# Three of the first tile's four repeat copies on VectorE and one on ScalarE, in a kernel that normalizes rows and writes each twice

## The chip, the cores and the metric

The kernel runs on one core of a Trainium2 chip. Its time is the device time of one execution in microseconds, and the median of several executions is given. A profiled execution also has a span, from the first to the last instruction that the profiler records; the time is a little longer than the span.

## The reference

```python
def setup_inputs():
    B, S, D = 8, 512, 2048
    R = 2
    return {
        "x": np.random.randn(B, S, D).astype(np.float32),
        "gamma": np.random.randn(D).astype(np.float32),
    }

def reference(x, gamma):
    B, S, D = x.shape
    x_rep = np.repeat(x, 2, axis=1)
    rms = np.sqrt((x_rep ** 2).mean(axis=-1, keepdims=True) + 1e-6)
    x_norm = x_rep / rms
    return (x_norm * gamma[None, None, :]).astype(np.float32)
```

Each of the 8 x 512 = 4096 rows of 2048 numbers is divided by its root mean square and multiplied by `gamma`, and the result is written twice, to two neighbouring rows of the output. The input is 33.55 MB, the output 67.11 MB, both in 32-bit floats.

## The kernel before

**Tiles.** The input is read in four loads. A load gives each of the 128 partitions 8 neighbouring rows (8.39 MB). It feeds two tiles of K = 4 rows a partition. The output of a tile is 8 rows a partition, since each row stands there twice, and leaves in one store of 8.39 MB. That makes 4 loads and 8 stores.

**Space.** One buffer `y` holds 24 rows a partition, in three parts of 8: `first` at 0, `second` at 8, `third` at 16. A load into row 4 fills the upper half of `first` and the lower half of `second`; a load into `third` fills that. Each tile is scaled from where it was loaded into rows 0, 2, 4 and 6 of the part that its store will read, and the copies then fill rows 1, 3, 5 and 7.

**Order.** The work is written out by hand, and each engine takes its instructions in the order of the program. `four(n, m, ...)` handles one group: two loads and four tiles with their stores. It is called twice, for loads 0 and 1 and for loads 3 and 2. All loads and stores are issued by SyncE on one queue, one after another, and SyncE waits in turn for what each of them needs: a store for the copies that fill its part, a load or a later tile's scaling for the store that still reads the part. In the first group both loads are issued at once; in the second they are issued as earlier stores land. In each group the queue then holds, in order, load, load, store, store, store, store.

**One tile.** ScalarE squares each row and sums it (`squares`, line 69), then takes the root for the tile or half of it (line 73). VectorE takes the reciprocal (line 82) and multiplies each row by it and by `gamma` in one instruction (`scale`, line 83). `repeat(to, k0, k1, copy)` (lines 88 to 90) copies rows k0 to k1 of the tile into the rows beside them with a single instruction of whichever engine it is given; its shape is (k1 - k0) rows of 2048. `store` (line 56) sends the 8 rows.

**Who copies.** In the first tile of a group (lines 103 to 107) the rows are squared and scaled in two halves; ScalarE copies rows 0 and 1, VectorE rows 2 and 3, and the first store follows. The second tile (lines 108 to 111) is scaled from its last row to its first; ScalarE copies rows 2 and 3, VectorE rows 0 and 1. Then ScalarE squares both tiles of the other load and makes their copies alone (lines 112 to 119). In the first group the second half's reciprocals are taken row by row (`at_once` = 1), in the second both at once.

**The end.** After the last group ScalarE waits until the last but one store has landed and then makes three copies on one partition (line 156); SyncE waits for the last store.

Of the kernel before, what the change touches and what calls it, by code (L numbers as in the profile page):

```python
# [1 line left out]

# [4 lines left out]


@with_exitstack
def kernel(  # L10
    ctx: ExitStack,
    tc: tile.TileContext,
    x: bass.AP,
    gamma: bass.AP,
    out: bass.AP,
):
    nc = tc.nc
    P = nc.NUM_PARTITIONS
    f32 = mybir.dt.float32
    Act = mybir.ActivationFunctionType  # L20
    Alu = mybir.AluOpType

    B, S, D = x.shape
    Bo, So, Do = out.shape
    R = So // S
    assert R == 2 and D == Do and B == Bo and So == S * R
    eps = 1e-6
    inv_d = 1.0 / float(D)


    K = 4
    N = B * S
    ntiles = N // (P * K)
    assert N % (P * K) == 0 and ntiles == 8
    H = 2
    x_t = x.rearrange("b s d -> (b s) d").rearrange("(n p k) d -> n p k d", p=P, k=H * K)
    out_t = out.rearrange("b s d -> (b s) d").rearrange("(n p h j) d -> n h p (j d)", p=P, h=H, j=K * R)

    singles = ctx.enter_context(tc.tile_pool(name="singles", bufs=1))
    rows = ctx.enter_context(tc.tile_pool(name="rows", bufs=1))  # L40
    junk = ctx.enter_context(tc.tile_pool(name="junk", bufs=1, space=bass.MemoryType.PSUM))
    small = ctx.enter_context(tc.tile_pool(name="small", bufs=4))

    y = nc.alloc_sbuf_tensor("y", [P, 3 * K * R, D], f32)
    first, second, third = 0, K * R, 2 * K * R

    def load(n, at):
        nc.sync.dma_start(out=y[:, at : at + H * K, :], in_=x_t[n])  # L50

    landed = [nc.alloc_semaphore(f"landed{h}") for h in range(H)]
    passed = nc.alloc_semaphore("passed")

    def store(n, h, to, own=False):
        dma = nc.sync.dma_start(
            out=out_t[n, h], in_=y[:, to : to + K * R, :].rearrange("p j d -> p (j d)")
        )
        if own:
            tc.no_tile_sem_insts.add(dma.ins.name)  # L60
            dma.then_inc(landed[h], 16)

    def squares(at, rows):

        n = len(rows)
        ss = small.tile([P, n], f32, name=f"ss{n}")
        for c, k in enumerate(rows):
            sq = junk.tile([P, D], f32, name="sq")
            nc.scalar.activation(  # L69
                out=sq[:], in_=y[:, at + k, :], func=Act.Square, accum_out=ss[:, c : c + 1]  # L70
            )
        rms = small.tile([P, n], f32, name=f"rms{n}")
        nc.scalar.activation(out=rms[:], in_=ss[:], func=Act.Sqrt, scale=inv_d, bias=eps_t[:])  # L73
        return rms

    def scale(at, to, rows, rms, at_once=K):
        n = len(rows)
        rstd = small.tile([P, n], f32, name=f"rstd{n}")
        for c, k in enumerate(rows):
            if c % at_once == 0:  # L80
                part = slice(c, min(c + at_once, n))
                nc.vector.reciprocal(out=rstd[:, part], in_=rms[:, part])  # L82
            nc.vector.scalar_tensor_tensor(  # L83
                out=y[:, to + R * k, :], in0=y[:, at + k, :], scalar=rstd[:, c : c + 1],
                in1=gamma_b[:], op0=Alu.mult, op1=Alu.mult,
            )

    def repeat(to, k0, k1, copy):
        y_r = y[:, to + R * k0 : to + R * k1, :].rearrange("p (k r) d -> p k r d", r=R)
        copy(out=y_r[:, :, 1, :], in_=y_r[:, :, 0, :])  # L90

    ctx.enter_context(tc.manual_schedule())

    half = K // 2
    up, down = list(range(K)), list(range(K - 1, -1, -1))

    def four(n, m, constants, at_once, last=False):


        load(n, first + K)  # L100
        constants()
        load(m, third)
        for rows, n_at_once in ((up[:half], half), (up[half:], at_once)):
            scale(first + K, first, rows, squares(first + K, rows), n_at_once)
        repeat(first, 0, half, nc.scalar.copy)
        repeat(first, half, K, nc.vector.tensor_copy)
        store(n, 0, first)
        scale(second, second, down, squares(second, down))
        repeat(second, half, K, nc.scalar.copy)
        repeat(second, 0, half, nc.vector.tensor_copy)  # L110
        store(n, 1, second)
        roots = [squares(third + h * K, up) for h in range(H)]
        scale(third, first, up, roots[0])
        repeat(first, 0, half, nc.scalar.copy)
        repeat(first, half, K, nc.scalar.copy)
        store(m, 0, first, last)
        scale(third + K, third, up, roots[1])
        repeat(third, 0, K, nc.scalar.copy)
        store(m, 1, third, last)

    gamma_b = singles.tile([P, D], f32, name="gamma_b")
    G, E = 16, 3
    C = D // G - E
    gamma_s = y[0:1, 0:2, :].rearrange("p k (c d) -> p (k c) d", c=G // 2)
    gamma_t = y[0:1, 2, :]
    eps_t = singles.tile([P, 1], f32, name="eps_t")

    def constants():
        nc.gpsimd.memset(eps_t, eps)  # L129

        nc.scalar.activation(out=gamma_s[0:1, 0, :1], in_=eps_t[0:1, :], func=Act.Sqrt)  # L131
        nc.scalar.dma_start(
            out=gamma_s[0:1, :, :C],
            in_=gamma[: G * C].rearrange("(p c d) -> p c d", p=1, c=G),
        )
        for c in range(E):
            at = G * C + c * G
            nc.scalar.dma_start(
                out=gamma_t[0:1, c * G : (c + 1) * G],
                in_=gamma[at : at + G].partition_broadcast(1),  # L140
            )
        nc.gpsimd.partition_broadcast(  # L142
            out_ap=gamma_b[:, : G * C].rearrange("p (c d) -> p c d", c=G),
            in_ap=gamma_s[0:1, :, :C],
        )
        nc.gpsimd.partition_broadcast(out_ap=gamma_b[:, G * C :], in_ap=gamma_t[0:1, : E * G])  # L146

    four(0, 1, constants, 1)
    four(3, 2, lambda: None, half, last=True)

    ctx.close()
    tc.close()
    tc.compile()
    nc.scalar.wait_ge(landed[0], 16).then_inc(landed[0], -16)  # L154
    for a, b in ((0, K), (K, 2 * K), (2 * K, 2 * K + 2)):
        done = nc.scalar.copy(out=y[0:1, a:b, :], in_=y[0:1, a:b, :])  # L156
    done.then_inc(passed, 1)
    nc.vector.wait_ge(passed, 1).then_inc(passed, -1)
    nc.sync.wait_ge(landed[1], 16).then_inc(landed[1], -16)


# [1 line left out]
_INS = ['x', 'gamma']  # L163
_OUTS = [((8, 1024, 2048), 'float32')]


# [23 lines left out]
```

## Time and profile before

| What | Value |
|---|---|
| median of 3 runs | 236.88 us (236.84 to 237.99) |
| profiled execution, time | 237.09 us |
| profiled execution, span | 235.8 us |
| VectorE busy | 84.4 us (36%) |
| ScalarE busy | 127.6 us (54%) |
| moved by DMA | 100.69 MB, mean 427 GB/s |
| read from HBM, written to it | 33.56 MB, 67.11 MB |
| DMA time from issue to landing, median | stores 24.9 us, loads of x 31.5 us |

How to read it. DVE is VectorE, ACT is ScalarE, SP is SyncE; SPq is SyncE issuing a transfer, and L90 is line 90 of the kernel. A group of instructions is given as line, engine, operation, output <- input with the shape as partitions x elements, and the count; then the busy time in us and the mean of one in ns; then the idle time of the engine just before them and what ended it. A line of the timeline begins with the start and the length in us; a line with x4 merges four instructions, and its length reaches to the end of the last. A line of the windows gives a stretch and its length, the busy time of DVE, ACT and POOL with their counts, the granted clock of TensorE, the share of the 16 DMA engines and the rate. That view books a DMA packet whole in the window in which it starts, so in a very short window the share can be over 1.

### The profile page before, as it was taken

How to read it: one execution, taken by the hardware profiler on the slowest of the kernel's cores; microseconds unless marked ns; L12 is line 12 of the kernel's file. 1: busy time of each engine (PE TensorE's matmuls, PEld its weight loads, DVE VectorE, ACT ScalarE, POOL GpSimd, SP SyncE). 2: the span in 40 equal slices, each digit the busy share in tenths (PEclk: the TensorE clock that was granted, in tenths of full speed). 3: DMA queues.
4: the chain of work that ended last, by engine and by line, in shares of the span. 5: the costliest groups of instructions: out<-in, count | busy, mean ns of one | idle time of the engine just before them, and what ended most of it. 6: DMA issues, size and time to landing. Idle time of an engine off the chain costs nothing. (4 is left out here: it accounts for less than half of the span.)

```text
span 235.8 us, 233 instructions
## 1 busy us (share of the span) xinstructions
DVE 84.4 (36%) x47; ACT 127.6 (54%) x89; POOL 2.9 (1%) x7
## 2 busy tenths in 40 slices
DVE  0000396594599500000000006937928993000000
ACT  2001989479999370000000039891999966502996
POOL 0120000000000000000000000000000000000000
DMA  9898988989898998989899898989889898989988
GB/s 356 357 534 356 534 356 356 534 356 534 356 523 368 411 478 356 534 356 534 356 445 445 356 534 356 534 356 511 378 378 511 356 534 356 523 367 467 423 356 357
DMA packets 1769, 100.69 MB, mean 427 GB/s; under 512 B 231, under 2 KB 231, under 8 KB 231
## 3 DMA queue, kind: packets, MB, share of 16 engines
q1 hardware_dynamic: 1728, 100.66, 99.0%
q14 instruction: 3, 0.02, 0.0%
q10 hardware_dynamic: 38, 0.01, 0.0%
HBM read 33.56 MB, written 67.11 MB: 427 GB/s over the span
## 5 line engine op out<-in xcount | busy, mean ns | idle before, releaser
L69 ACT ACTIVATE sq<-y 128x2048 f32<-128x2048 f32 x32 | 60.1, 1878 | 73.0 <-DMA y<-in_x_dram 72.4
L83 DVE SCALAR_TENSOR_TENSOR y<-y,rstd,gamma_b 128x2048 f32<-128x2048 f32 x32 | 73.8, 2348 | 1.7 <-DMA out_dram<-y 1.2
L90 ACT COPY y<-y 128x4096 f32<-128x4096 f32 (+1 forms) x10 | 42.6, 4283 | 19.2 <-DVE y L83 18.5
L82 DVE RECIPROCAL rstd<-rms 128x4 f32<-128x4 f32 (+2 forms) x11 | 1.8, 168 | 110.1 <-ACT rms L73 110.1
L156 ACT COPY y<-y 1x8192 f32<-1x8192 f32 (+1 forms) x3 | 17.4, 5876 | 13.0 <-ACTq L154 13.0
L90 DVE COPY y<-y 128x4096 f32<-128x4096 f32 x4 | 9.2, 2294 | 0.1
L69 ACT ACTIVATION_READ_ACCUMULATOR sq<-y 128x1 f32 x32 | 6.0, 186 | 0.0
L73 ACT ACTIVATE rms<-ss,eps_t 128x4 f32<-128x4 f32 (+1 forms) x10 | 3.0, 297 | 0.3
L142 POOL PARTITION_BROADCAST gamma_b<-y x1 | 2.2, 2244 | 9.9 <-DMA y<-in_gamma_dram 9.9
L131 ACT ACT_TABLE_LOAD x1 | 1.3, 1283 | 0.7 <-PEq L174 0.7
L146 POOL PARTITION_BROADCAST gamma_b<-y x1 | 0.3, 323 | 10.1 <-DMA y<-in_gamma_dram 10.1
L131 ACT ACTIVATE y<-eps_t 1x1 f32<-1x1 f32 x1 | 0.2, 202 | 0.0
L174 POOL MEMSET const-uint8-127<- 128x1 uint8 x1 | 0.1, 102 | 0.0
L129 POOL MEMSET eps_t<- 128x1 f32 x1 | 0.1, 98 | 0.3 <-POOLq L174 0.3
L174 POOL MEMSET const-bfloat16-1.0<- 128x1 bf16 x1 | 0.1, 101 | 0.0
L174 POOL MEMSET const-float32-0.0<- 128x1 f32 x1 | 0.1, 98 | 0.2 <-issue 0.2
L174 POOL MEMSET const-float32-1.0<- 128x1 f32 x1 | 0.1, 98 | 0.0
## 6 DMA issues: line engine op xcount, KB each, us to landing
out_dram<-y SPq DMA_DIRECT2D x8, 24.9
y<-in_x_dram SPq DMA_DIRECT2D x4, 31.5
y<-in_gamma_dram ACTq DMA_DIRECT2D x3, 0.1 KB
y<-in_gamma_dram ACTq DMA_DIRECT2D x1, 7.8 KB, 8.3
```

Of the source, the lines that this page charges most:

```text
L69: nc.scalar.activation(out=sq[:], in_=y[:, at + k, :], func=Act.Square, accum_out=ss[:, c : c + 1])
L73: nc.scalar.activation(out=rms[:], in_=ss[:], func=Act.Sqrt, scale=inv_d, bias=eps_t[:])
L82: nc.vector.reciprocal(out=rstd[:, part], in_=rms[:, part])
L83: nc.vector.scalar_tensor_tensor(out=y[:, to + R * k, :], in0=y[:, at + k, :], scalar=rstd[:, c : c + 1], in1=gamma_b[:], op0=Alu.mult, op ...
L90: copy(out=y_r[:, :, 1, :], in_=y_r[:, :, 0, :])
L129: nc.gpsimd.memset(eps_t, eps)
L131: nc.scalar.activation(out=gamma_s[0:1, 0, :1], in_=eps_t[0:1, :], func=Act.Sqrt)
L142: nc.gpsimd.partition_broadcast(out_ap=gamma_b[:, : G * C].rearrange("p (c d) -> p c d", c=G), in_ap=gamma_s[0:1, :, :C],)
L146: nc.gpsimd.partition_broadcast(out_ap=gamma_b[:, G * C :], in_ap=gamma_t[0:1, : E * G])
L156: done = nc.scalar.copy(out=y[0:1, a:b, :], in_=y[0:1, a:b, :])
L174: nc = _bacc.Bacc("TRN2", target_bir_lowering=False, num_devices=1)
```

## The change

In `four`, which both groups run, ScalarE copies one row of the first tile (row 0) where it copied two, and VectorE copies three (rows 1 to 3) where it copied two. The number of instructions stays: one copy on each engine. The copies of all other tiles, the order of the program, and the loads and stores stay as they are.

```diff
         for rows, n_at_once in ((up[:half], half), (up[half:], at_once)):
             scale(first + K, first, rows, squares(first + K, rows), n_at_once)
-        repeat(first, 0, half, nc.scalar.copy)
-        repeat(first, half, K, nc.vector.tensor_copy)
+        repeat(first, 0, 1, nc.scalar.copy)
+        repeat(first, 1, K, nc.vector.tensor_copy)
         store(n, 0, first)
```

## The prediction

> **What bounds the kernel now.** I read the page first, then the DMA queues, the windows around two moments, the timeline of VectorE and SyncE there, and the groups by form.
>
> ```profile
> DMA  9898988989898998989899898989889898989988
> q1 hardware_dynamic: 1728, 100.66, 99.0%
> L82 DVE RECIPROCAL rstd<-rms 128x4 f32<-128x4 f32 (+2 forms) x11 | 1.8, 168 | 110.1 <-ACT rms L73 110.1
> ```
>
> The transfers set the time. All loads and stores stand on one queue, q1, and its packets fill 99.0% of 16 engines' span; VectorE alone waits 110 us. No compute can shorten that; compute can only lengthen it, by letting the queue run dry. A store can be late in four places per group, so the question is which one is nearly late now. The windows show it; the columns that matter are the DMA share and the GB/s, and this view books a packet whole at the moment it starts.
>
> ```profile
> 1.70:2.30 0.60, 0.00 (x0) 0.51 (x2) 0.00 (x0) 1.00 5.26 1748
> 39.40:41.30 1.90, 0.00 (x0) 1.87 (x3) 0.00 (x0) 1.00 0.00 0
> 41.30:41.90 0.60, 0.00 (x0) 0.57 (x3) 0.00 (x0) 1.00 4.04 1748
> 155.50:157.40 1.90, 0.00 (x0) 1.87 (x3) 0.00 (x0) 1.00 0.08 34
> 157.40:158.10 0.70, 0.00 (x0) 0.67 (x3) 0.00 (x0) 1.00 3.47 1498
> ```
>
> In 0.6 us 1748 GB/s are 1.05 MB, which is 16 packets of 64 KB, one on each engine. The first line is the start of the first load. Until 41.3 us 16.8 MB have started, which are the two loads of the first group, so the burst at 41.30 to 41.90 is the first packet of the group's first store: the engines come free from the loads there, the first at 41.35. By the same count (8.39 MB a transfer) the burst from 157.44 us is the first packet of the second group's first store. Now when those stores are issued, and what comes just ahead:
>
> ```profile
> 34.54 2.35 DVE L83 SCALAR_TENSOR_TENSOR y<-y,rstd,gamma_b 128x2048 f32<-128x2048 f32 x1
> 36.93 2.29 DVE L90 COPY y<-y 128x4096 f32<-128x4096 f32 x1
> ...
> 153.21 2.29 DVE L90 COPY y<-y 128x4096 f32<-128x4096 f32 x1
> ```
>
> ```profile
> 0.73 0.85 SPq L50 DMA_DIRECT2D y<-in_x_dram  x2
> 39.29 48.30 SPq L56 DMA_DIRECT2D out_dram<-y  x4
> 100.25 20.05 SPq L50 DMA_DIRECT2D y<-in_x_dram  x2
> 155.56 48.25 SPq L56 DMA_DIRECT2D out_dram<-y  x4
> ```
>
> VectorE's copy ends at 39.22 and 155.50, and the store is issued 0.06 to 0.07 us later (39.29, 155.56): VectorE's copy is the last thing the store waits for. The issue leads the engines' coming free by 41.35 - 39.29 = 2.06 us, and by 157.44 - 155.56 = 1.88 us. How much lead an issue needs is seen once, at the start: issue at 0.73, first packets from 1.73, so 1.00 us; that issue took 0.42 us where a store's takes 0.35, so 0.93 for a store. The slack in the two places is therefore about 2.06 - 0.93 = 1.13 and 1.88 - 0.93 = 0.95 us, and a longer VectorE copy goes straight against it.
>
> **The change, part by part.** Its cost hangs on these rows:
>
> ```profile
> L83 DVE SCALAR_TENSOR_TENSOR y<-y,rstd,gamma_b 128x2048 f32<-128x2048 f32 x32 | 73.8, 2348 | 1.7 <-DMA out_dram<-y 1.2
> L90 ACT COPY y<-y 128x4096 f32<-128x4096 f32 x8 | 28.6, 3600 | 11.1 <-DVE y L83 10.4 <-DVE rstd L82 0.7
> L90 ACT COPY y<-y 128x8192 f32<-128x8192 f32 x2 | 14.0, 7017 | 8.0 <-DVE y L83 8.0
> L90 DVE COPY y<-y 128x4096 f32<-128x4096 f32 x4 | 9.2, 2294 | 0.1
> ```
>
> *ScalarE's copy, two rows to one, twice.* Two rows take 3.60 and four 7.02, so a row is 1.71 and one alone 1.89 us. It needs only row 0, which VectorE has finished by 29.7, so the 0.73 us idle before it goes too: it runs from about 31.3 to 33.2 in place of 32.05 to 35.65. ScalarE's next squares start 2.3 us sooner (about 2.4 from 148.35 in the second group), and so does the second store's chain. Worth nothing: that store is ready at 55.8 now and the engines want it only at 60.7, and the first store waits for VectorE, not for ScalarE.
>
> *VectorE's copy, two rows to three, twice.* No copy of three rows, nor of any odd number, is in the trace. A small VectorE instruction costs 0.154 us (the reciprocal of 128x1), so a two-row copy is 0.15 fixed and 2.14 of streaming. Lower end: time goes by elements at the rate of the two-row copy, 0.15 + 1.5 x 2.14 = 3.36 (3.44 with nothing fixed). Upper end: an odd count loses the fast rate, 0.15 + 3 x 2.14 = 6.57. Between them: a two-row copy (2294 ns) takes no longer than the multiply of one row (2348 ns), so the engine seems to move two rows side by side, at one element each a cycle; a third row then has no partner and needs a pass of its own, 0.15 + 2 x 2.14 = **4.43 us**. I take this: it explains why two rows cost what one does without supposing that one row could be cut in two.
>
> [...]
>
> *The first store, first group.* Copy from 36.93 to 41.36, issue at 41.43, first packet 0.93 later at 42.36; the engines come free at 41.35: **1.0 us** idle on each. *Second group.* Copy 153.21 to 157.64, issue 157.70, packet 158.63 against 157.44: **1.2 us**. The first stall delays the second group's loads, the compute that waits for them, and the end of its loads alike, so the second adds to it: 2.2 us.
>
> *Restarting the engines.* The first 16 packets of the kernel are 3.16 us long (5.26 x 0.60 us, one for each engine), those of the first store 2.42 (4.04 x 0.60): a dry queue may cost 0.73 more at each restart. Those first packets were a load's, read from HBM with nothing ahead; every store in the trace came into a running queue. Bounds 0 and 0.73 each; with no row nearer to one, I take half, 0.37 twice.
>
> [...]
>
> *What is behind the waits.* Behind the first store on SyncE stand only later stores and loads. On VectorE the next reciprocal waits for ScalarE's root, which now comes at about 41.7, just after the copy at 41.36: no new wait. Store 3 of a group needs VectorE to overwrite what store 1 has read (idle to 61.66 now, so later by the stall): that ScalarE copy ends near 75.9 instead of 76.2, and the queue wants store 3 past 80. The end moves with the queue: ScalarE's last three copies (216.47 to 233.91) start when the last but one store has landed, and the last store lands near 235.4 now.
>
> Sum: 1.0 + 1.2 + 0.73 = +2.9 us. The profiled execution took 237.09 (235.8 span and 1.3 around it), so 240.0; the median of the runs shown is 0.21 lower, 236.88, which gives **239.8**. Around this, with the copy at 4.43: issue to packet is at least the issue's own 0.34, which takes 1.2 off and with no restart cost leaves +1.0; both restarts in full make +3.7. So 237.9 to 240.6.
>
> **The rivals.**
> *Three rows at the full rate* (not slower). Copy 3.36 to 3.44; issue at 40.36 to 40.44 and 156.63 to 156.71; packets at 41.29 to 41.37 and 157.56 to 157.64, against 41.35 and 157.44: stalls of 0.0 and 0.1 to 0.2. Time 237.1, with one restart 237.8. It decides for copies under about 3.5 us. For it: 0.56 ns an element in the two-row copy. Against: nothing shows what pairs the elements, rows or neighbours.
> *An odd count falls to one element at a time.* Copy 6.57, each stall 2.14 longer than in my case: 3.1 + 3.3 + 0.73 = +7.2, time 244.1 (243.4 to 244.8). For it: the multiply shows the engine at 1.15 ns an element. Against: the same line and form of copy runs at 0.56.
> *ScalarE's shorter work makes it faster.* That could be only if the queue had gaps to close, and it has 1.7 us at the head, 0.4 at the tail and hardly any between: 236.8.
>
> **How the numbers follow.** 4.43 us: 0.66. Full rate: 0.16. Single rate: 0.14. No effect or a gain by something unseen: 0.04. The forecast is the first case's, 239.8, whose own range is 237.9 to 240.6. Taking in the full rate and leaving out the single rate and the last, 236.8 to 240.9 holds 0.8. A measurement of this kernel tells about 0.5% (1.2 us) from no change. Slower: nearly all of the first case, all of the third and a little of the second, 0.81. Same: most of the second and the low edge of the first, 0.17. Faster: 0.02.
>
> **What the profile after would show.** A VectorE copy of 128x6144, twice, at 4.43 us (3.4 or 6.6 for the rivals); VectorE's busy time at 88.7, ScalarE's at 124.2. The first store issued at about 41.4, and windows with no packet start for 1.0 us longer before the burst, and 1.2 in the second group; q1's share near 97.8%; the first packets of those stores at 2.4 to 3.2 us. I would be wrong if the copy is 3.4 us long, if the issue needs much less lead into a queue that has just been running, or if a restarted engine catches up.

## The result and the profile after

The change makes the kernel slower: 239.45 us (median of 5 runs, 239.41 to 239.54) against 237.12 us for the kernel before (5 runs, 236.84 to 237.99), a ratio of 1.0093 with a 95% interval of 1.0074 to 1.0112, or 2.3 us. The forecast was 239.8. The profiled execution took 239.54 us with a span of 238.2.

The page after, busy times and the queue of all transfers:

```profile
DVE 88.7 (37%) x47; ACT 124.4 (52%) x89; POOL 2.9 (1%) x7
q1 hardware_dynamic: 1728, 100.66, 98.3%
```

The same bytes in the same number of packets, and a share of 98.3% where it was 99.0 and the forecast 97.8. The groups by form of the kernel after show the new copies:

```profile
L90 DVE COPY y<-y 128x6144 f32<-128x6144 f32 x2 | 8.8, 4424 | 0.1
L90 DVE COPY y<-y 128x4096 f32<-128x4096 f32 x2 | 4.6, 2294 | 0.1
L90 ACT COPY y<-y 128x2048 f32<-128x2048 f32 x2 | 3.8, 1882 | 0.0
```

Three rows take VectorE 4.424 us, 2.13 more than two. Its timeline and that of SyncE after:

```profile
36.95 4.42 DVE L90 COPY y<-y 128x6144 f32<-128x6144 f32 x1
...
154.80 4.42 DVE L90 COPY y<-y 128x6144 f32<-128x6144 f32 x1
```

```profile
0.72 0.85 SPq L50 DMA_DIRECT2D y<-in_x_dram  x2
41.44 46.84 SPq L56 DMA_DIRECT2D out_dram<-y  x4
101.53 20.11 SPq L50 DMA_DIRECT2D y<-in_x_dram  x2
159.29 46.82 SPq L56 DMA_DIRECT2D out_dram<-y  x4
```

The first store of the first group is issued at 41.44 where it was 39.29, 0.07 us after the copy's end. The windows after, around both places (stretch, its length, busy times, clock, DMA share, GB/s; a packet counts where it starts):

```profile
38.60:39.30 0.70, 0.70 (x1) 0.67 (x3) 0.00 (x0) 1.00 3.46 1498
39.30:42.25 2.95, 2.79 (x3) 2.13 (x3) 0.00 (x0) 1.00 0.00 0
42.25:42.50 0.25, 0.25 (x1) 0.00 (x0) 0.00 (x0) 1.00 9.83 4194
156.80:157.30 0.50, 0.50 (x1) 0.47 (x3) 0.00 (x0) 1.00 4.84 2097
157.30:160.10 2.80, 2.51 (x3) 2.11 (x3) 0.00 (x0) 1.00 0.00 0
160.10:160.30 0.20, 0.20 (x1) 0.00 (x0) 0.00 (x0) 1.00 12.28 5243
```

The bursts of 16 packets follow each other every 2.42 us while the queue is full; here 2.95 and 2.80 us pass with no packet starting, where it was 1.90 in the kernel before. A stall is the time from the end of an engine's last packet of one transfer to the start of its first packet of the next. Its mean over the 16 engines is 1.03 us ahead of the first group's first store and 0.78 us ahead of the second's: 1.81 us together. The last packet ends at 237.83 us after the start and at 235.35 in the kernel before, 2.48 later. In the mean over the engines the end moves by 2.78 (234.94 to 237.72), since they now end 0.20 us apart instead of 0.63. So 0.7 to 1.0 us are not in the stalls. Most of it is at one place, the last store packets of the first group and the first load packets of the second. Before, then after:

```profile
116.05:116.95 0.90, 0.00 (x0) 0.00 (x0) 0.00 (x0) 1.00 2.79 1165
118.75:119.35 0.60, 0.00 (x0) 0.00 (x0) 0.00 (x0) 1.00 4.12 1748
```

```profile
117.30:118.60 1.30, 0.00 (x0) 0.00 (x0) 0.00 (x0) 1.00 2.35 807
120.15:121.00 0.85, 0.00 (x0) 0.00 (x0) 0.00 (x0) 1.00 3.08 1234
```

Each line holds 16 packets, one for each engine (the rate times the length is 1.05 MB), so the share times the length is the mean length of one. The last store packets are 2.35 x 1.30 = 3.06 us long, 2.51 before; the first load packets 2.62, 2.47 before. That is 0.7 us in a place where the change has no instruction. The store packets behind each stall are a little longer too, by 0.04 to 0.10 us a store.

### The profile page after: what moved, and what is told of

Read it like the earlier page. It is cut to its first block, busy times and chain, and to the rows that moved or that the text cites. A ratio compares the mean times of both kernels' runs of the same rounds, so it can differ in the third digit from the quotient of the medians.

```text
span 238.2 us, 232 instructions
## 1 busy us (share of the span) xinstructions
DVE 88.7 (37%) x47; ACT 124.4 (52%) x89; POOL 2.9 (1%) x7
## 3 DMA queue, kind: packets, MB, share of 16 engines
q1 hardware_dynamic: 1728, 100.66, 98.3%
## 5 line engine op out<-in xcount | busy, mean ns | idle before, releaser
L90 ACT COPY y<-y 128x4096 f32<-128x4096 f32 (+2 forms) x10 | 39.4, 3943 | 23.8 <-DVE y L83 23.8
L90 DVE COPY y<-y 128x6144 f32<-128x6144 f32 (+1 forms) x4 | 13.4, 3359 | 0.1
```

## The experiments

Two questions: is the store's lateness the cause, and is VectorE's length what makes it late; and what are the 0.7 us at the switch from stores to loads. The runs came in three groups of four, each beside its own runs of the kernel before (237.18, 237.25 and 236.91 us). Stalls are means over the 16 engines; "last packets" is the mean length of the last store packets ahead of the second group's first load. Both come from the one profiled execution of each run, while the times are medians. The kernel before ranges from 236.83 to 238.31 us over these groups, and the one execution of it that was profiled took 237.09.

| Run | stall, group 1 | stall, group 2 | last packets | time | over before | ratio, 95% interval |
|---|---|---|---|---|---|---|
| before | 0 | 0 | 2.51 | 237.12 | | |
| after | 1.03 | 0.78 | 3.06 | 239.45 | 2.3 | 1.0093 (1.0074 to 1.0112) |
| e1 | 0.17 | 0.50 | 3.19 | 238.87 | 1.7 | 1.006 (1.004 to 1.0079) |
| e2 | 0.18 | 0.11 | 3.16 | 239.11 | 1.9 | 1.0072 (1.0053 to 1.0091) |
| e3 | 1.06 | 0.78 | 3.07 | 240.39 | 3.2 | 1.0128 (1.0108 to 1.0148) |
| e4 | 1.06 | 0.77 | 3.03 | 239.40 | 2.2 | 1.0086 (1.0067 to 1.0104) |
| e5 | 0.90 | 0 | 3.06 | 238.76 | 1.5 | 1.0065 (1.0045 to 1.0084) |
| e6 | 0 | 0.80 | 2.66 | 237.94 | 0.7 | 1.0031 (1.0016 to 1.0047) |
| e7 | 2.37 | 2.09 | 3.09 | 242.82 | 5.6 | 1.0234 (1.021 to 1.0257) |
| e8 | 0.97 | 0.80 | 3.10 | 239.47 | 2.2 | 1.0091 (1.0073 to 1.011) |
| e9 | 0.17 | 0.02 | 2.95 | 239.00 | 2.1 | 1.0078 (1.006 to 1.0096) |
| e10 | 0.65 (second store) | 0 | 3.04 | 238.49 | 1.6 | 1.006 (1.0042 to 1.0077) |
| e11 | 0.18 | 0.06 | 3.11 | 238.85 | 1.9 | 1.0076 (1.0057 to 1.0094) |
| e12 | 1.09 | 0.90 | 3.02 | 239.51 | 2.6 | 1.0101 (1.0084 to 1.0118) |

### e1: the same three rows, with the halves of a row as the outer dimension

```diff
-        repeat(first, 1, K, nc.vector.tensor_copy)
+        repeat_halves(first, 1, K, nc.vector.tensor_copy)
+    def repeat_halves(to, k0, k1, copy):
+        y_r = y[:, to + R * k0 : to + R * k1, :].rearrange("p (k r) (c d) -> p c k r d", r=R, c=2)
+        copy(out=y_r[:, :, :, 1, :], in_=y_r[:, :, :, 0, :])
```

> The same three rows in one VectorE copy, but its pattern runs over the two halves of a row first and over the three rows second, so that the outermost count is even. Late store (my theory: three rows cost two passes, the copy is 1 us longer than its elements need, and the first store of each group comes late by that): the copy drops from 4.42 to about 3.36 us, the first stores are issued about 1.05 us sooner than with the change, the queue hardly stalls, time 237.0 to 237.4, within 0.3 us of before. Rival, rows on VectorE: what costs is that a third row goes through VectorE at all, beside the transfers, however long it takes: time stays near 239.4. Rival, early ScalarE: what costs is that ScalarE's later work starts sooner: near 239.4 too, since ScalarE's copy stays at one row.

The group of this copy, SyncE's stores and a window at the first of them, in e1:

```profile
L94 DVE COPY y<-y 128x6144 f32<-128x6144 f32 x2 | 6.7, 3360 | 0.1
```

```profile
40.30 47.23 SPq L56 DMA_DIRECT2D out_dram<-y  x4
...
158.21 47.25 SPq L56 DMA_DIRECT2D out_dram<-y  x4
```

```profile
41.20:41.72 0.52, 0.28 (x2) 0.17 (x1) 0.00 (x0) 1.00 4.72 2017
116.20:117.50 1.30, 0.00 (x0) 0.00 (x0) 0.00 (x0) 1.00 2.45 807
```

The copy moves the same 6144 elements in 3.360 us with two halves outermost, instead of 4.424 with three rows outermost: the order of the pattern cost the extra 1.06. The stores are issued 1.1 us sooner and the stalls shrink from 1.81 to 0.67 us in all. But the time fell by only 0.6 us, to 238.87, and not to the 237.0 to 237.4 that my theory said. The late store explains the stalls; it does not explain the rest, which stays whole with a first stall of only 0.17 us (last packets 2.45 x 1.30 = 3.19).

### e2: two rows and one row

```diff
-        repeat(first, 1, K, nc.vector.tensor_copy)
+        repeat(first, 1, 3, nc.vector.tensor_copy)
+        repeat(first, 3, K, nc.vector.tensor_copy)
```

> VectorE copies rows 1 and 2 in one instruction and row 3 in one of its own. Late store: 2.29 us and, split in two halves, about 1.22 us for the single row, together 3.45 to 3.55: one instruction more, and yet 0.9 us less than the one copy of 4.42; time 237.1 to 237.5. If a single row were also moved at one element a cycle, it would take 2.29, the pair 4.5, and the time would be 239.5. Rivals, rows on VectorE and early ScalarE: near 239.4.

```profile
L90 DVE COPY y<-y 128x4096 f32<-128x4096 f32 x4 | 9.2, 2289 | 0.1
L90 DVE COPY y<-y 128x2048 f32<-128x2048 f32 x2 | 2.4, 1220 | 0.0
```

These groups of e2 bear the copies out: a row alone takes 1.220 us, about half of two rows' 2.289, which is 0.60 ns an element where two rows take 0.56 and the multiply 1.15; the pair takes 3.42 in the timeline. Two instructions are 1 us shorter than the one. The time, 239.11, again misses the 237.1 to 237.5, by at least 1.6 us, with stalls of 0.18 and 0.11. About 0.3 us of that is the fetch of instructions that is told under e3: one DMA engine ends 0.34 us behind the next.

### e3 and e12: VectorE's half of the change alone

```diff
-        repeat(first, 0, 1, nc.scalar.copy)
+        repeat(first, 0, half, nc.scalar.copy)
         repeat(first, 1, K, nc.vector.tensor_copy)
```

In e12 also the first group takes both reciprocals of the second half at once, one instruction fewer on VectorE:

```diff
-    four(0, 1, constants, 1)
+    four(0, 1, constants, half)
```

> VectorE's half of the change alone: VectorE copies rows 1 to 3 in one instruction, and ScalarE goes on copying rows 0 and 1 (row 1 is written twice with the same values), so ScalarE's work starts no sooner than before. Late store: the copy is 4.42, the first stores are as late as with the change, time 239.2 to 239.6. Rival, early ScalarE: back to 237.1.

> VectorE's half of the change alone, as in the run that took 240.39, with one reciprocal fewer in the first group. Theory of the fetch (one more instruction or wait on an engine moves an 8 KB fetch of instructions ahead of the end, into the last stores, where it holds one DMA engine up by 0.9 us): the fetch goes back behind the last store, and the time is that of the change, 239.2 to 239.6. Rival, ScalarE's later work is worth 0.9 us: it stays at 240.2 to 240.5.

Without ScalarE's half the stalls are those of the change (1.06 and 0.78), so ScalarE's earlier start is neither the cause nor a help there. Yet e3 took 240.39, 0.9 us more than the change. The DMA queues of e3 in the stretch 205 to 215 us show a packet that most other runs have only behind the last store, and the windows at the start of its last store:

```profile
q14 instruction: 1, 0.01, 0.2%
```

```profile
218.20:218.45 0.25, 0.00 (x0) 0.00 (x0) 0.00 (x0) 1.00 9.11 3932
218.45:219.20 0.75, 0.00 (x0) 0.00 (x0) 0.00 (x0) 1.00 0.00 0
219.20:219.30 0.10, 0.00 (x0) 0.00 (x0) 0.00 (x0) 1.00 1.52 655
```

Fifteen engines start the last store within 0.25 us, the sixteenth 0.75 us behind them, and the store ends with that one. At 213.8 us an 8 KB fetch of instructions took 0.31 us of an engine, with a longer store packet on either side of it (2.69 and 2.77 us). e12 has one VectorE instruction fewer; its fetch comes at 237.9, its 16 engines start the last store together, and it takes 239.51:

```profile
218.40:218.70 0.30, 0.00 (x0) 0.00 (x0) 0.00 (x0) 1.00 8.10 3495
```

So the 0.9 us of e3 belonged to the fetch, and not to ScalarE's work. e2 and e7, which have an instruction more in each group, have this fetch at 212 and 216 us too. The traces bear it out: e2, e3 and e7 hold 64 instructions of VectorE, waits counted, and all other runs 62 or 63. In e3, where two engines' copies both write row 1, the two more are waits. The engine with the fetch ends 0.78 us behind the next one in e3 and in e7.

### e4: four rows on VectorE

```diff
-        repeat(first, 0, 1, nc.scalar.copy)
-        repeat(first, 1, K, nc.vector.tensor_copy)
+        repeat(first, 0, K, nc.vector.tensor_copy)
```

> VectorE copies all four rows of the first tile in one instruction, ScalarE none. Late store: four rows are two passes as three are, so the copy takes 4.42 us like that of three, and the time is that of the change, 239.2 to 239.7. If three rows took 4.42 because of a rate per element (0.72 ns), four would take 5.9 and the time would be about 242.3. Rival, rows on VectorE: a price per row moved, so two rows cost twice the 2.3 us: 241.7.

```profile
L90 DVE COPY y<-y 128x8192 f32<-128x8192 f32 x2 | 8.9, 4428 | 0.1
```

Four rows take 4.428 us and three 4.424. The time is that of the change (239.40). A price per row or per element is out: VectorE takes as long for three rows as for four.

### e5 and e6: the change in one group only; e8: the change again

```diff
-        repeat(first, 0, 1, nc.scalar.copy)
-        repeat(first, 1, K, nc.vector.tensor_copy)
+        own = K // 2 if last else 1
+        repeat(first, 0, own, nc.scalar.copy)
+        repeat(first, own, K, nc.vector.tensor_copy)
```

That is e5; e6 has `own = 1 if last else K // 2`, and e8 is the change as it is.

> The change in the first group only. Late store: one stall of about 1.0 us ahead of the first group's first store, none in the second group; time up by 1.0 to 1.4 us over before. If only the second group's stall reached the end (the first being made up later, since the second group's loads wait for stores anyway): no change from before.

> The change in the second group only. Late store: one stall of 0.8 to 1.2 us ahead of the second group's first store; time up by 0.8 to 1.2 us, and with the first group alone it adds to the 2.3 us of the whole change. If the change's cost lay in the first group and in what follows from it: no change from before.

> The change itself, beside the three others on the same chip: 239.2 to 239.7, and the trace shows whether the last packets ahead of the second group's first load are longer again (3.05 us on average for the last of each engine, 2.42 elsewhere), which is 0.6 us of the change's time that the two stalls do not explain. If they are at 2.4 to 2.5 here, that part was a property of one execution.

First group alone +1.5 us, second alone +0.7, both +2.2: they add. But stalls of nearly one length (0.90 and 0.80) cost twice as much in the first group as in the second. The last store packets of e5, then of e6:

```profile
117.20:118.50 1.30, 0.00 (x0) 0.00 (x0) 0.00 (x0) 1.00 2.35 807
```

```profile
115.80:117.00 1.20, 0.00 (x0) 0.00 (x0) 0.00 (x0) 1.00 2.22 874
```

3.06 us against 2.66, and 2.51 in the kernel before. e5 pays at the switch to the second group's load, 77 us behind its stall; e6, which stalls only after the last load, has no such switch to come and pays its stall. e8 shows the long packets again (3.10), so they are no accident of one execution. The other side is less certain: e6 has no stall in its first group, and yet five of its 16 engines have a last packet of 2.8 to 3.0 us. Its profiled execution (237.69) was one of its fastest (237.66 to 238.63). Whether the slower executions of e6, or of the kernel before, have the long packets too, no trace shows.

### e7: later still

```diff
         repeat(first, 1, K, nc.vector.tensor_copy)
+        repeat(first, 3, K, nc.vector.tensor_copy)
```

> The change, and behind VectorE's copy of three rows one more of row 3 alone (the same values written again), in both groups. It only makes the first stores later, by about 1.15 us each. Late store: past the slack every us of lateness is a us of time, so 2 x 1.15 on top of the change: 241.5 to 242.0. If a late store were partly made up (by a faster restart, or by the queue's later slack): less than 241.0.

The stalls grew by 1.34 and 1.31 us, 2.65 in all, which from the change gives 242.1; it took 242.82, and the 0.7 us more go with the fetch of instructions at 216 us in its trace. Nothing of the lateness is made up later. The last packets, 3.09, are no longer than after a stall of 0.17: that part does not grow with the stall.

### e9: a store that is late within the slack

```diff
+        if not last:
+            nc.vector.tensor_copy(
+                out=y[:, first + 7, : 3 * D // 4], in_=y[:, first + 6, : 3 * D // 4]
+            )
         store(n, 0, first)
```

This is the kernel before with that copy, and with the first group's two reciprocals taken at once.

> The kernel before, with VectorE's last work ahead of the first group's first store made about 0.7 us longer by a copy of three quarters of a row (and one reciprocal fewer, so that it issues as many instructions as before). The store is issued at about 40.0 us, and its first packet could start at 40.9, just ahead of the engines' coming free at 41.0 to 41.6. Theory of the lost lead (an engine that is never dry reads ahead of what it writes, so later hiccups hide; once it has run dry they show, about 0.7 us at the next switch from stores to loads): no stall, so no loss anywhere, the last packets ahead of the second group's first load stay at 2.4 to 2.7 us, time 236.9 to 237.5. Rival, the time follows the lateness of the store, dry queue or not: 0.7 us of lateness costs 0.5 us or more, 237.8 or above.

It missed its mark. The added copy took 0.96 us, the store was issued at 40.19, its first packet started at 41.15 where the engines came free from 40.93: a stall of 0.17 us, as in e1. So it could not tell the two theories apart; a store that is late without any stall was not tried again. What it adds is one more price: a mean stall of 0.17 us in one group, and 2.1 us. It also says something on the lead, beside e6, whose first group is that of the kernel before. The first group's stores of e6, e9 and e11:

```profile
39.44 48.06 SPq L56 DMA_DIRECT2D out_dram<-y  x4
40.19 47.35 SPq L56 DMA_DIRECT2D out_dram<-y  x4
40.23 47.52 SPq L56 DMA_DIRECT2D out_dram<-y  x4
```

In e1, e2, e9 and e11 the first store was issued 0.74 to 0.95 us ahead of the first engine's coming free. Pairing ends and starts in order of time, every engine paused, by 0.06 to 0.23 us, and the mean is 0.17 or 0.18 in all four. In e6 it was issued 1.53 us ahead, and no engine paused. So the lead that costs nothing lies somewhere between 0.95 and 1.53 us here.

### e10: another store late, and e11: the shortest stall in one group only

```diff
         repeat(second, 0, half, nc.vector.tensor_copy)
+        if not last:
+            repeat(second, 0, half, nc.vector.tensor_copy)
+            repeat(second, 0, half, nc.vector.tensor_copy)
         store(n, 1, second)
```

That is e10, on the kernel before, with the first group's two reciprocals at once. e11 is e1 with the three rows in the first group only.

> The kernel before, with two more copies of rows on VectorE ahead of the first group's second store (the same values again), so that this store, and not the first, is late by some 0.2 to 0.6 us. Lost lead: whichever store runs the queue dry, the price is the stall and then about 0.7 us at the switch to the second group's first load, where the last store packets are 3.0 to 3.2 us on average; time up by 1.0 to 1.8 us. Rival, the later loss belongs to the first tile and how its copies are shared: only the stall, up by 0.2 to 0.6 us.

> Only the first group has three rows on VectorE, and in the form that takes 3.36 us: a stall of 0.2 us or less ahead of the first store, none in the second group. Lost lead: the price is a step and not a slope: 0.1 to 0.2 us of stall cost 1.0 to 1.4 us in all, 238.2 to 238.6, close to what 0.9 us of stall cost (238.76). Rival, the time follows the length of the stall: 237.3 to 237.6.

The last store packets of e10, then of e11:

```profile
116.90:118.20 1.30, 0.00 (x0) 0.00 (x0) 0.00 (x0) 1.00 2.34 807
```

```profile
116.20:118.00 1.80, 0.00 (x0) 0.00 (x0) 0.00 (x0) 1.00 1.73 583
```

3.04 and 3.11 us. In e10 the first store is on time and the copies are shared as before; the second store stalls by 0.65 us, and the long packets come all the same, +1.6 us in all. So they belong to the queue's having run dry, and not to this tile. In e11 0.18 us of stall cost 1.9 us, above what I expected (1.0 to 1.4) and about as much as e5's 0.90: the medians are 238.85 and 238.76, and the differences (1.9 and 1.5) go against different runs of the kernel before. A stall in the first group thus has a price like a step, 1.5 to 2.1 us for 0.17 to 0.90 us of it, and beyond that it goes by its length (e7: 2.65 us more of stall, 3.37 us more of time than the change, 0.7 of it with the fetch). The profiled execution of e11, the slowest of its six, took 239.50, and its engines end 1.7 us later in the mean than those of the kernel before. I can put numbers on about 1.6 of that: 0.18 in the stall, 1.0 at the switch with the load's first packets and a pause of 0.15 ahead of them, 0.2 in slightly longer store packets behind the stall, and 0.25 in slower packets of its next load. Its last engine ends 2.46 us later, because its engines end up to 1.5 us apart (236.3 to 237.8), those of e5 0.6; why the short stalls spread the engines so is open.

## Why the prediction was right, and where it was not

*What bounds the kernel, and the place.* Right. The queue bounds it (a share of 98.3%), VectorE's copy is what the first store waits for (issued 0.07 us after it), and the loss begins there.

*The copy at 4.43 us.* Right (4.424): four rows take the same (4.428), and three with two halves outermost 3.360. The reading behind it, two rows side by side and the third in a pass of its own, was an estimate from two durations, 2.294 us for a two-row copy and 2.348 for the multiply of one row. It fits three rows and four. It does not fit the single row, which by it would take as long as two and takes 1.220 us in e2, half of that. What VectorE pairs inside one copy no trace shows.

*ScalarE's half worth nothing.* Right: e4, where ScalarE copies no row of the tile, and e12, where it copies two, are within 0.3 us of the change.

*The first stall, 1.0 us.* Right in size, with some luck: 1.03 in the mean, from 1.24 on the engine that is free first to 0.77 on the last. The sum was for the engine that is free first; that one waited 1.24, because the loads ended 0.30 us sooner in this execution (41.05 instead of 41.35). The issue needed 0.85 us to its first packet, where I took 0.93. The slack of 1.13 us was put too long: it took a lead of 0.93 for enough, and with 0.74 to 0.95 us for the first engine, and 1.3 to 1.5 for the last, every engine still paused (e1, e2, e9, e11).

*The second stall, 1.2 us.* Too long: 0.78. The shorter lead is 0.1 of it. For the rest I took the time of the engine that is free first and held it fixed against the group's compute. The compute starts behind the last engine's end of the load (0.36 us in the kernel before, 139.11 against 138.75; 0.37 in the kernel after, 140.71 against 140.34), and the stall ahead had drawn the engines together: they end that load 0.38 us apart instead of 0.65, so the second load ended about 0.26 us later against the start of the compute than before.

*The restarts, 0.37 us each, as part of the first packets.* The size was near, the step wrong. The first store packets behind the stall are 2.46 us long, not 2.8 (9.83 x 0.25 in the window after), so restarting a store costs 0.04 us. In its place the runs show a later price: about 0.7 us at the switch from the first group's stores to the second group's loads, in all twelve runs whose first group had run dry (last packets 2.95 to 3.19) and not, or much less, in the one trace each of the kernel before and of e6 (2.51, 2.66), and some 0.05 to 0.1 us a store behind each stall. So the 0.73 that I added for restarts came nearly in full, but elsewhere and from the first stall alone: that this term fits is luck. My sum of 2.9 is 0.6 above the measured 2.3, and 0.4 of that is the second stall.

*The rival of the full rate, 237.1 to 237.8.* Its condition was tried in e1 and e2, and its time was wrong: copies of 3.36 and 3.42 us gave 238.87 and 239.11. I priced a stall by its length and took a stall of 0.1 us for nothing. The point from which it decides, a copy of about 3.5 us, was wrong too: at 3.36 us the kernel is already 0.6% slower.

*The single rate* is out, by the copy's length (4.424 us, not 6.57). *A gain from ScalarE* is out: no run was faster than before.

What makes the price come late is not shown. The theory of the lost lead, put in e9's expectation, rests on no trace, since no run looked at the reads by themselves. What fits it is that the long packets at the switch exceed 2.42 by 0.6 us, as the kernel's very first load packets do (3.06 after), that they do not grow with the stall, and that behind the switch the stores of e5 and e10 run at 2.42 again. What does not fit is e6, where five engines have such packets without a stall ahead of them.

## What to carry to other kernels

Where one full queue sets the time, find the transfer with the shortest lead and count every instruction ahead of its issue against that lead, and leave a margin: here a lead of 0.95 us was too short and one of 1.53 enough, and a stall of 0.17 us cost as much as one of 0.9. Try another order of a VectorE copy's pattern: here three rows outermost took 4.424 us, as long as four (4.428), and the same three rows with two halves outermost 3.360. And do not judge a stall at its own place only; what it cost came partly 77 us later, about 0.7 us where the queue turned from stores to loads.

## What was not expected

- A dry queue that restarts with stores shows almost no cost there (2.46 us for the first packets against 2.42) but about 0.7 us at its next load.
- An 8 KB fetch of instructions, 0.31 us long, came between the data. In e3 the store packets on either side of it were 2.69 and 2.77 us long, one of the 16 engines ended 0.78 us behind the next, and the kernel was 0.9 us slower than the change; with one VectorE instruction fewer (e12) the fetch came at 237.9, behind the last store.
- The time from a store's issue to its first packet is not one number. It is 0.84 or 0.85 us where the issue comes no more than 0.3 us ahead of the first engine's coming free (the change itself, the second groups of e1 and e2), and 0.96 to 1.17 us in the first groups of e1, e2, e9 and e11, which were issued further ahead; there the first packet starts 0.20 to 0.23 us after that engine comes free. The slack is shorter than the first load of the trace suggests.
